# A hybrid attention and convolution layer on one core: the order of work at the end of each pair of column blocks, and one pattern of quads

## The chip, the cores and the metric

The kernel runs on one core of a Trainium2 chip. The metric is the device time of one execution in microseconds. A core has five engines that matter here: TensorE (PE) multiplies, VectorE (DVE) and ScalarE (ACT) work on elements, GpSimd (POOL) and SyncE (SP) issue transfers. Each engine takes its instructions from one queue, strictly in order: an instruction that waits holds up all that stand behind it.

## The reference

One layer on 256 tokens of width 4096, in float32, batch 1:

```python
u = rmsnorm(h, norm_gain)
proj = u @ w_in                                   # 4096 x 16384
q, k, v, z_a, hc, b_gate, c_gate, z_c = split(proj)   # each 2048 wide
attn  = moba_attention(q, k, v, rel_bias) * silu(z_a)          # 16 heads of 128
conv  = b_gate * short_conv(c_gate * hc, conv_w) * silu(z_c)   # causal, width 3, by channel
mixed = concatenate([attn, conv])
out   = rmsnorm(h + mixed @ w_out, final_gain)    # w_out 4096 x 4096
```

The attention's blocks are 256 long, and so is the sequence: each query sees the keys of its own block alone. What is left is causal attention over 256 tokens with a bias by distance.

## The kernel before

**Products.** 128 tokens are the rows of one matmul's output, so there are two token halves. The input projection has 32 column blocks of 512, taken two at a time: 16 pairs (numbers 0 to 15). Pairs 0 to 7 give q and k, then v and z_attn, in turn for four groups of heads; pairs 8 to 15 give h and C, then z_conv and B, for four groups of channels. The output projection adds 4 pairs (16 to 19). A pair goes through the 4096 contraction rows in 16 **quads** of 256 rows. The raw weights of a quad are 256 rows x two blocks of 512 columns: a tile `raw` of 128 x 2048, 1 MB.

A quad is one of two kinds. An **eight-quad** (`P` in a pattern) multiplies two token halves x two row halves x two column blocks: eight products. A **seven-quad** (`S`) uses Strassen's seven products instead: four of them take the raw blocks, three take sums of blocks, which L593 and L594 form on DVE in a tile `sum` of 128 x 1536. For the seven-quad, the sums of the activations stand ready in the tiles `k`. The first of the sums, block one plus block two, is formed in DRAM by a copy and an adding transfer that POOL issues (L528, L529), some quads ahead.

**Three passes.** Every operand is split into a high part, rounded to the format fp32r, and a low part, the rest. ACT casts the high part of the weights (`hi`, L611); DVE subtracts it for the low part (`lo`, L613). A product is three matmuls of 128 x 128 by 512 columns: high times high (L685), low activations times high weights (L686), high activations times low weights (L688). The low part is thus needed last, and within a unit all high products stand ahead of the low ones.

**Units.** A seven-quad is two units: the *raw unit* (12 matmuls) and the *sum unit* (9 matmuls). An eight-quad is one unit of 24 matmuls. `split(u + 2)` prepares the unit after next while unit u multiplies; three buffers each exist for `raw`, `hi` and `lo`. The program states what depends on what, and a scheduler sets the order in each engine's queue from it; it may move an instruction ahead of another of the same engine where nothing forbids it.

**The order of a pair.** `PATS` and `KIND` say which quads of a pair are seven-quads. Pairs 2 to 10, 12 and 14 have pattern `t`, which is `PSSPSSSPSSPSSSPP`: ten seven-quads in runs of two, three, two and three, the last at place 13, then two eight-quads.

**Accumulators.** PE writes into eight banks, 1 to 8 (odd pairs swap the names). The seven-quads' products go into all eight: banks 2, 3, 4 and 8 are the four results, and the banks 1, 5, 6 and 7 belong to shared products that have to be added to the results later. After the last seven-quad of a pair these four banks are done, and `early` evacuates them:

```python
es = cur["es"] = ep.tile([P, 4, B], F32, name="es")
nc.scalar.copy(es[:, 0], acc[1])                                                    # L395, ACT
nc.vector.tensor_tensor(es[:, 1], acc[6], es[:, 0], ALU.add)                        # L396, DVE
nc.vector.tensor_tensor(es[:, 2], acc[7], es[:, 1], ALU.add)                        # L397, DVE
nc.vector.tensor_tensor(es[:, 1::2], acc[5][:, None, :].to_broadcast([P, 2, B]), es[:, 1:3], ALU.subtract)  # L398, DVE
```

**What runs in the banks set free.** While the last two eight-quads fill banks 2, 3, 4 and 8, smaller work goes into banks 1, 5, 6 and 7, each piece counted in by products (`tasks_of`). In pairs 1, 3, 5 and 7 it is turning q and k (L300 on PE, L302 on ACT), the scores (L307 on PE, L313 the exponential on ACT) and turning the probabilities (L322, L324). In pairs 2, 4, 6 and 8 it is the values (L331 on PE, L336 on DVE) and turning what comes of them (L357 on PE, L358 on ACT). In pairs 10, 12 and 14 it is the convolution: PE turns the two inputs of a channel group (L377, L379), ACT takes the first tap, DVE the two others (L383) and the product (L385). In pair 17 it is one load of ACT's table for the square root (L655, L656). At the pair's end the results are taken out of banks 2, 3, 4 and 8 (L408 for the input pairs), with what `early` left in `es` added.

**The end of the program.** The last output pair finishes one token half after the other: `last_end` adds a quarter (L483) and squares it (L485), `summed` reduces the squares, and `finish` scales the half's 4096 columns and stores them (from L250 on).

Of the kernel before, what the change touches and what calls it, by code (L numbers as in the profile page):

```python
# [10 lines left out]
F32 = mybir.dt.float32  # L11
# [3 lines left out]
ALU = mybir.AluOpType  # L15
AX = mybir.AxisListType

P = 128
# [10 lines left out]
B = 512  # L29
# [8 lines left out]

PATS = {"7": "PSPSPSPSPSPSPSPP", "8": "PSPSSPSPSSPSPSPP", "n": "PSPSPSPSSPSPSPSP",
        "9": "PSPSSPSSPSSPSSPP", "m": "PSPSSPSPSSPSPSSP", "e": "PSPSPSPSPSPSSPPP", "f": "PSPSSPSPSSPSSPPP",  # L40
        "t": "PSSPSSSPSSPSSSPP"}
KIND = "01tttttt" "ttt9t9t9" "099e"
RING = 3
SLOT = 4
# [27 lines left out]
N_PAIRS = 16  # L72
# [11 lines left out]
def of(pattern):  # L84
    seven = SEVEN[:pattern.count("S")]
    eight = dict.fromkeys(EIGHT + SEVEN[len(seven):])
    return in_order(pattern, seven, [q for q in eight if q not in seven]), set(seven)
# [3 lines left out]
ORDERS, SEVENS = zip(*([(FIRST0, {8, 10, 12, 14}), (SECOND, {4, 6, 8, 10, 12, 14})]  # L91
                       + [of(PATS[k]) for k in KIND[2:N_PAIRS]]
                       + [(FIRST, {8, 6, 10, 12, 14})] + [of(PATS[k]) for k in KIND[N_PAIRS + 1:]]))
# [21 lines left out]
def hymba_layer(ctx: ExitStack, tc: tile.TileContext, xT, xres, gain, w, convw, wout,  # L115
                relb, onehot, fgain, out):
    nc = tc.nc
# [274 lines left out]
    def early(acc):  # L392

        es = cur["es"] = ep.tile([P, 4, B], F32, name="es")
        nc.scalar.copy(es[:, 0], acc[1])  # L395
        nc.vector.tensor_tensor(es[:, 1], acc[6], es[:, 0], ALU.add)  # L396
        nc.vector.tensor_tensor(es[:, 2], acc[7], es[:, 1], ALU.add)  # L397
        nc.vector.tensor_tensor(es[:, 1::2], acc[5][:, None, :].to_broadcast([P, 2, B]), es[:, 1:3], ALU.subtract)  # L398

    def part(t, n):  # L400
        return cur["es"][:, 2 * (1 - t) + n]
# [46 lines left out]
    def gain_load(p):  # L448
        gf = fin["gf"] = ep.tile([P, 8, P], F32, name="c", bufs=2).rearrange("p n c -> p (n c)")
        nc.sync.dma_start(gf, bass.AP(tensor=fgain.tensor, offset=fgain.offset + p * 2 * B,  # L450
                                      ap=[[0, P], [1, 2 * B]]))
# [4 lines left out]
    def pair_of(t):  # L456
        return cur["es"][:, 2 * (1 - t):2 * (2 - t)].rearrange("p n c -> p (n c)")

    def out_early(p, acc):
        early(acc)  # L460
        if p == NDP - 1:
            for t in (0, 1):
                added(p, t)
        gain_load(p)
# [6 lines left out]
    def added(p, t):  # L471
        nc.vector.tensor_tensor(row_of(p, t), row_of(p, t), pair_of(t), ALU.add)
# [34 lines left out]


    quads = QUADS
    raws, xrs, halves, sums, kept_at = {}, {}, {}, {}, []  # L510
    t1_d = [dram.tile([COPY, P * B // COPY], F32, name=f"t1_{j}") for j in range(T1S)]
    t1s, t1_next = {}, [0]

# [59 lines left out]
    def split(u):  # L573

        n, kind, at, products = units[u]
        first = u == 0 or units[u - 1][0] != n
        p, i, q = quads[n]
        if first:
            load(n + AHEAD)
            if p == 0:  # L580
                x_parts(q, xrs.pop(q))
            if q in SEVENS[p]:
                raw = raws[n].rearrange("p (b c) -> p b c", b=4)

                k = sum(x in SEVENS[p] for x in ORDERS[p][:i])
                if k % 2 and N_PAIRS <= p < N_PAIRS + NDP - 1:
                    t = fin["hg"][:, 0, D - 3 * B:].rearrange("p (b c) -> p b c", b=3)
                else:
                    t = (cur["pool"] if k % 2 and p < N_PAIRS else wp).tile([P, 3, B], F32, name="sum")
                sums[n] = t  # L590
                if n not in PRE:
                    nc.vector.tensor_tensor(raw[:, 0], raw[:, 0], raw[:, 1], ALU.add)
                nc.vector.tensor_tensor(t[:, 0], raw[:, 0], raw[:, 2], ALU.subtract)  # L593
                nc.vector.tensor_tensor(t[:, 1:], raw[:, 1::2], t[:, :1].to_broadcast([P, 2, B]), ALU.subtract)  # L594
        src = raws[n] if kind == "raw" else sums[n].rearrange("p b c -> p (b c)")
        m = len(products) * B
        src = src[:, at * B:at * B + m]
        if p == N_PAIRS + NDP - 1 and i >= KEPT:

            spot = ORDERS[p][2 * len(kept_at):]  # L600
            kept_at.append(u)
            hi, lo = (kt.tile([P, SIZES[k], 2, P], F32R, name=f"k{k}")
                      .rearrange("p n h c -> p (n h c)") for k in spot[:2])
        else:
            hi = wp.tile([P, SLOT * B], F32R, name="hi", bufs=RING)
            lo = wp.tile([P, SLOT * B], F32R, name="lo", bufs=RING)
        step = B if n < LEAD else m if m < 4 * B else LO * B
        for a in range(0, m, step):
            half = step if step < 2 * HI * B else HI * B
            for b in range(a, a + step, half):  # L610
                nc.scalar.copy(hi[:, b:b + half], src[:, b:b + half])  # L611
            c = slice(a, a + step)
            nc.vector.tensor_tensor(lo[:, c], src[:, c], hi[:, c].bitcast(F32), ALU.subtract)  # L613
        halves[u] = hi, lo


    def tasks_of(p):

        t = {}

        def put(at, f, *a):
            t.setdefault(at, []).append((f, a))
        if p < 8 and p % 2:
            for at, f, j, n in ((4, turn, 0, 1), (5, turn, 1, 6), (7, scores, 0, 7), (8, scores, 1, 5),
                                (9, turn, 2, 1), (11, probs, 0, 6), (12, turn, 3, 7), (13, scores, 2, 5),
                                (14, probs, 1, 1), (15, scores, 3, 6)):
                put(at, f, p // 2 * HG + j, n)
        elif 2 <= p <= 8:
            for j, (at, banks) in enumerate(zip(((4, 8), (6, 10), (8, 12), (11, 14)),
                                                ((1, 7), (6, 1), (5, 5), (7, 6)))):  # L630
                for f, a_, n in zip((values, mixed), at, banks):
                    put(a_, f, (p - 2) // 2 * HG + j, n)
        elif p == N_PAIRS + 1:

            put(8, root_table)
        elif p in (10, 12, 14):
            for j in range(4):
                put(4 + 3 * j, conv, (p - 10) // 2 * 4 + j, (7, 5, 1, 6)[j])
        return t
# [23 lines left out]
    acc = {}  # L663
# [27 lines left out]
    for u, (n, kind, at, products) in enumerate(units):  # L691
        p, i, q = quads[n]
# [10 lines left out]
        hi, lo = halves.pop(u)  # L703
# [28 lines left out]
        if i == last_seven[p]:  # L732
            assert not tasks
            behind, tasks = 0, tasks_of(p)
            if p < N_PAIRS:
                early(acc)
                rows = (rQ if p < 8 and p % 2 == 0 else rT, rT)
                for j, (_, t, c) in enumerate(ENDS):
                    tasks.setdefault(TS[j] if i < NQ - 2 else 4 + j, []).append((scaled, (part(t, c), rows[c][:, t:t + 1])))
            else:  # L740
                out_early(p - N_PAIRS, acc)

            split(u + 2)
        if (p, i) == (N_PAIRS + NDP - 2, NQ - 1):
# [9 lines left out]
        if (p, i + 1) in RAISE:  # L754
            q = RAISE[p, i + 1]
            raised[q] = x_again(q) if p < N_PAIRS else m_load(q)
        if (p, i) in RAISE:
            q = RAISE[p, i]
# [92 lines left out]
```

## Time and profile before

| | |
|---|---|
| time, median of 3 runs | 1708.32 us (1707.31 to 1709.75) |
| the profiled execution's own time | 1707.3 us |
| its span in the trace | 1705.5 us |
| PE busy | 1680.9 us, 7529 matmuls and transposes |
| DVE busy | 1562.0 us, 1348 instructions |
| ACT busy | 1064.8 us, 1182 instructions |
| POOL busy | 137.9 us, 173 instructions |
| moved by DMA | 458.91 MB, 269 GB/s on average |
| granted TensorE clock | 0.998 |

How to read the lines that follow. A row of the timeline gives the start in microseconds from the span's beginning, the length, the engine, the line of the kernel, the operation, what is written and read (a tile's name; `p` is a bank), the shape, the type, and how many alike follow one another; the length is from the first one's start to the last one's end. In square brackets stands the idle time of the engine just before, and what ended it. A matmul's recorded length overlaps the next one's: what a matmul takes of PE is read from one start to the next. Groups of instructions are rows of the page: the idle time before them, with the number of cases and the longest, stands behind what released them.

### The profile page before, as it was taken

What the parts mean: (1) busy time and instruction counts of PE and PEld (TensorE: products, weight loads), DVE (VectorE), ACT (ScalarE), POOL (GpSimd) and SP (SyncE); (2) the same over time, 40 slices, a digit from 0 to 9 for tenths busy, and PEclk for the clock granted to TensorE, in tenths of its full rate; (3) what the DMA queues carried; (4) which work ended last, traced back from release to release, by engine and by line L of the source; (5) the groups of instructions that cost most, each with busy time, mean ns of one, the idle gap of its engine ahead of it and who ended that gap; (6) DMA issues with size and microseconds to landing.
All of it is one profiled execution on the core that took longest, in us unless ns stands there. A gap on an engine that the chain in (4) does not pass through costs nothing.

```text
span 1705.5 us, 20704 instructions
## 1 busy us (share of the span) xinstructions
PE 1680.9 (99%) x7529; PEld 1382.5 (81%) x7529; DVE 1562.0 (92%) x1348; ACT 1064.8 (62%) x1182; POOL 137.9 (8%) x173
## 2 busy tenths in 40 slices
PE   9999999999999999999999999999999999999997
PEld 7888778888787878788888788888888888878886
DVE  7989988998899989899999999899989999989887
ACT  6856755675567556765665566656665656556563
POOL 0000000000000001010100001000100000001000
PEclk9999999999999999999999999999999999999999
DMA  9878788878797979797979798798888888889884
GB/s 335 296 249 290 228 263 261 270 249 287 242 288 231 282 244 282 230 283 245 292 257 291 239 281 271 250 292 268 272 261 274 283 308 294 275 276 277 284 292 171
DMA packets 119042, 458.91 MB, mean 269 GB/s; under 512 B 15499, under 2 KB 20396, under 8 KB 96940
## 3 DMA queue, kind: packets, MB, share of 16 engines
q1 hardware_dynamic: 94604, 413.66, 66.9%
q0 software_dynamic: 24048, 43.79, 15.9%
q8 instruction: 59, 0.97, 0.2%
q14 instruction: 43, 0.35, 0.1%
q10 hardware_dynamic: 288, 0.15, 0.0%
HBM read 448.36 MB, written 96.73 MB: 320 GB/s over the span
## 4 chain that ended last, share of the span: by engine, by line
PE 92%; DVE 4%; ACT 2%; issue 1%; DMA 1%; SPq 0%; DVEq 0%; ACTq 0%
PE p L685 30%; PE p L686 30%; PE p L688 30%; DVE lo L613 1%; DMA raw<-in_w_dram 1%; ACT hi L611 1%; DVE y L383 0%; ACT bt L313 0%; DVE es L397 0%; ACT L313 0%; DVE es L396 0%; DVE es L398 0%; PE p L307 0%; PE p L322 0%; PE p L331 0%
## 5 line engine op out<-in xcount | busy, mean ns | idle before, releaser
L685 PE MATMUL p<-hi,k 128*128 128x512 f32 x2359 | 918.5, 391 | 5.5 <-DVE mt L385 3.8
L686 PE MATMUL p<-hi,k 128*128 128x512 f32 x2359 | 915.9, 390 | 0.0
L613 DVE TENSOR_TENSOR lo<-raw,hi 128x2048 fp32r<-128x2048 f32 (+1 forms) x323 | 725.2, 2248 | 57.6 <-ACT hi L611 57.4
L611 ACT CAST hi<-raw 128x1024 fp32r<-128x1024 f32 (+1 forms) x638 | 635.3, 1042 | 209.9 <-PE p L686 139.9
L688 PE MATMUL p<-lo,k 128*128 128x512 f32 x2359 | 634.6, 392 | 0.0
L685 PEld LDWEIGHTS p<-hi,k 128*128 128x128 f32 x2359 | 442.8, 188 | 102.4 <-ACT hi L611 4.4
L686 PEld LDWEIGHTS p<-hi,k 128*128 128x128 f32 x2359 | 443.1, 188 | 91.9 <-issue 0.6
L688 PEld LDWEIGHTS p<-lo,k 128*128 128x128 f32 x2359 | 440.5, 188 | 88.8
L611 ACT CAST hi<-sum 128x1536 fp32r<-128x1536 f32 x167 | 247.5, 1482 | 279.6 <-DVE sum L594 211.6
L613 DVE TENSOR_TENSOR lo<-sum,hi 128x1536 fp32r<-128x1536 f32 x167 | 292.8, 1753 | 16.6 <-ACT hi L611 15.0
L529 POOL DMA_DIRECT2D t<-in_w_dram x137 | 112.6, 822 | 1208.3 <-DMA t<-in_w_dram 880.3
L594 DVE TENSOR_TENSOR sum<-raw,sum 128x1024 f32<-128x1024 f32 x167 | 204.2, 1223 | 3.4
L593 DVE TENSOR_TENSOR sum<-raw 128x512 f32<-128x512 f32 x167 | 114.5, 686 | 0.6 <-DMA raw<-in_wout_dram 0.4
L396 DVE TENSOR_TENSOR es<-p,es 128x512 f32<-128x512 f32 x20 | 13.8, 691 | 41.6 <-PE p L688 31.9
L404 ACT ACTIVATE es<-es,rT 128x512 f32<-128x512 f32 x56 | 39.5, 721 | 14.4 <-DVE es L398 12.1
L529 POOL DMA_DIRECT2D t<-in_wout_dram x30 | 24.6, 821 | 293.9 <-DMA t<-in_wout_dram 227.7
L395 ACT COPY es<-p 128x512 f32<-128x512 f32 x20 | 11.7, 587 | 48.7 <-PE p L688 48.6
L611 ACT CAST hi<-hg 128x1536 fp32r<-128x1536 f32 x10 | 14.8, 1481 | 25.7 <-DVE hg L594 20.9
L175 DVE TENSOR_TENSOR k<-c,k 128x128 fp32r<-128x128 f32 (+3 forms) x42 | 25.5, 627 | 3.4 <-ACT k L174 3.4
L174 ACT CAST k<-c 128x128 fp32r<-128x128 f32 (+3 forms) x42 | 22.9, 567 | 3.5 <-DVE c L171 3.5
L398 DVE TENSOR_TENSOR es<-p,es 128x1024 f32<-128x1024 f32 x20 | 24.4, 1220 | 0.2
L171 DVE TENSOR_TENSOR c<-c 128x128 f32<-128x128 f32 x76 | 18.8, 287 | 0.1
(112 smaller groups left out, 525.3 us busy)
## 6 DMA issues: line engine op xcount, KB each, us to landing
raw<-in_w_dram SPq DMA_DIRECT2D x117, 1024.0 KB, 6.9
raw<-in_w_dram SPq DMA_DIRECT2D x137, 768.0 KB, 5.9
raw<-t SPq DMA_DIRECT2D x167, 256.0 KB, 3.6
t<-in_w_dram SPq DMA_DIRECT2D x137, 256.0 KB, 6.0
t<-in_w_dram POOLq DMA_DIRECT2D x137, 256.0 KB, 6.1
raw<-in_wout_dram SPq DMA_DIRECT2D x34, 1024.0 KB, 6.1
raw<-in_wout_dram SPq DMA_DIRECT2D x30, 768.0 KB, 6.4
t<-in_wout_dram SPq DMA_DIRECT2D x30, 256.0 KB, 7.0
```

The lines of the kernel that those rows point to most:

```text
L174: nc.scalar.copy(dst[:, :, 0], c)
L175: nc.vector.tensor_tensor(dst[:, :, 1], c, dst[:, :, 0].bitcast(F32), ALU.subtract)
L398: nc.vector.tensor_tensor(es[:, 1::2], acc[5][:, None, :].to_broadcast([P, 2, B]), es[:, 1:3], ALU.subtract)
L404: nc.scalar.activation(e, e, AF.Copy, scale=r)
L529: nc.gpsimd.dma_start(by_rows(t1), rest[:, :B], accum_op=ALU.add)
L593: nc.vector.tensor_tensor(t[:, 0], raw[:, 0], raw[:, 2], ALU.subtract)
L594: nc.vector.tensor_tensor(t[:, 1:], raw[:, 1::2], t[:, :1].to_broadcast([P, 2, B]), ALU.subtract)
L611: nc.scalar.copy(hi[:, b:b + half], src[:, b:b + half])
L613: nc.vector.tensor_tensor(lo[:, c], src[:, c], hi[:, c].bitcast(F32), ALU.subtract)
L685: nc.tensor.matmul(acc[b_], a, h_, start=s0, stop=False)
L686: nc.tensor.matmul(acc[b_], b, h_, start=False, stop=False)
L688: nc.tensor.matmul(acc[b_], a, l_, start=False, stop=s1)
```

## The change

Three things are altered; no instruction is added or removed on any engine.

1. In every seven-quad both sums (L593, L594) are put ahead of the raw unit's low part, by keeping the second sum and the low part in the order in which the program states them. (Lines of the changed kernel from here on: 592, 593, 612 for the cast, 614 for the low part.)
2. `split` remembers the last cast and the last low part of each unit. `early` is issued behind those of the unit that follows the last seven-quad (the first of the two eight-quads): on ACT L395 stands behind that unit's cast, on DVE L396 to L398 behind its low part.
3. Pattern `t` has its run of two and its second run of three exchanged: `PSSPSSSPSSSPSSPP`. The ten seven-quads and the six eight-quads are the same in number; the last seven-quad is still at place 13, with one seven-quad ahead of it instead of two.

```diff
-        "t": "PSSPSSSPSSPSSSPP"}
+        "t": "PSSPSSSPSSSPSSPP"}
...
-    def out_early(p, acc):
-        early(acc)
+    def out_early(p):
...
-                nc.vector.tensor_tensor(t[:, 1:], raw[:, 1::2], t[:, :1].to_broadcast([P, 2, B]), ALU.subtract)
+                made = nc.vector.tensor_tensor(t[:, 1:], raw[:, 1::2], t[:, :1].to_broadcast([P, 2, B]),
+                                               ALU.subtract)
+                tc.keep_in_program_order(made)
...
-                nc.scalar.copy(hi[:, b:b + half], src[:, b:b + half])
+                cast = nc.scalar.copy(hi[:, b:b + half], src[:, b:b + half])
             c = slice(a, a + step)
-            nc.vector.tensor_tensor(lo[:, c], src[:, c], hi[:, c].bitcast(F32), ALU.subtract)
+            low = nc.vector.tensor_tensor(lo[:, c], src[:, c], hi[:, c].bitcast(F32), ALU.subtract)
+            if kind == "raw" and q in SEVENS[p]:
+                tc.keep_in_program_order(low)
         halves[u] = hi, lo
+        ends[u] = cast.ins, low.ins
...
         if i == last_seven[p]:
             assert not tasks
             behind, tasks = 0, tasks_of(p)
+            with tc.issue_after(ends[u + 1][0]), tc.issue_after(ends[u + 1][1]):
+                early(acc)
             if p < N_PAIRS:
-                early(acc)
...
             else:
-                out_early(p - N_PAIRS, acc)
+                out_early(p - N_PAIRS)
```

**DVE at the end of pair 2.** `lo_2055` is the low part of the last seven-quad's sum unit, `lo_2070` and `lo_2106` are those of the two eight-quads behind it, `es` is the evacuation, and the rows of L336 are the heads' values. Before:

```order
L613 TENSOR_TENSOR lo_2055<-sum_2034,hi_2054 128x1536
L396 TENSOR_TENSOR es_2095<-p6_1653,es_2095 128x512
L336 SCALAR_TENSOR_TENSOR am_2144<-p1_2140,st_1471,z_1570 128x128
L397 TENSOR_TENSOR es_2095<-p7_1656,es_2095 128x512
L336 SCALAR_TENSOR_TENSOR am_2144<-p1_2140,st_1471,z_1570 128x128
L398 TENSOR_TENSOR es_2095<-p5_1635,es_2095 128x2x512
L336 SCALAR_TENSOR_TENSOR am_2154<-p6_2150,st_1482,z_1570 128x128 x2
L613 TENSOR_TENSOR lo_2070<-raw_1996,hi_2069 128x2048
```

In the changed kernel:

```order
L614 TENSOR_TENSOR lo_2055<-sum_2034,hi_2054 128x1536
L614 TENSOR_TENSOR lo_2070<-raw_1983,hi_2069 128x2048
L396 TENSOR_TENSOR es_2095<-p6_1653,es_2095 128x512
L397 TENSOR_TENSOR es_2095<-p7_1656,es_2095 128x512
L398 TENSOR_TENSOR es_2095<-p5_1635,es_2095 128x2x512
L336 SCALAR_TENSOR_TENSOR am_2144<-p1_2140,st_1471,z_1570 128x128 x2
L336 SCALAR_TENSOR_TENSOR am_2154<-p6_2150,st_1482,z_1570 128x128
L614 TENSOR_TENSOR lo_2106<-raw_2032,hi_2105 128x2048
```

The low part of the first eight-quad has gone from behind the evacuation to ahead of it, and the three instructions of the evacuation stand together, without the first head's values between them.

**DVE at the end of pair 12**, from the first two channel groups' products (L385 of `mt_8573`) to those of the other two (`mt_8633`). `sum_8597`, `lo_8601` belong to the first seven-quad of the next pair. Before:

```order
L385 TENSOR_TENSOR mt_8573<-p5_8579,y_8584 128x256
L593 TENSOR_TENSOR sum_8597<-raw_8527 128x512
L613 TENSOR_TENSOR lo_8601<-raw_8527,hi_8600 128x2048
L594 TENSOR_TENSOR sum_8597<-raw_8527,sum_8597 128x1024
L383 SCALAR_TENSOR_TENSOR y_8629<-p1_8624,cw_71,y_8629 128x255
L383 SCALAR_TENSOR_TENSOR y_8644<-p6_8639,cw_71,y_8644 128x255
L383 SCALAR_TENSOR_TENSOR y_8629<-p1_8624,cw_71,y_8629 128x254
L383 SCALAR_TENSOR_TENSOR y_8644<-p6_8639,cw_71,y_8644 128x254
L385 TENSOR_TENSOR mt_8633<-p1_8624,y_8629 128x256
L385 TENSOR_TENSOR mt_8633<-p6_8639,y_8644 128x256
```

In the changed kernel:

```order
L385 TENSOR_TENSOR mt_8573<-p5_8579,y_8584 128x256
L592 TENSOR_TENSOR sum_8597<-raw_8527 128x512
L383 SCALAR_TENSOR_TENSOR y_8629<-p1_8624,cw_71,y_8629 128x255
L593 TENSOR_TENSOR sum_8597<-raw_8527,sum_8597 128x1024
L614 TENSOR_TENSOR lo_8601<-raw_8527,hi_8600 128x2048
L383 SCALAR_TENSOR_TENSOR y_8629<-p1_8624,cw_71,y_8629 128x254
L383 SCALAR_TENSOR_TENSOR y_8644<-p6_8639,cw_71,y_8644 128x255
L385 TENSOR_TENSOR mt_8633<-p1_8624,y_8629 128x256
L383 SCALAR_TENSOR_TENSOR y_8644<-p6_8639,cw_71,y_8644 128x254
L408 SCALAR_TENSOR_TENSOR s_8654<-p3_8030,rT_69,es_8522 128x512
L385 TENSOR_TENSOR mt_8633<-p6_8639,y_8644 128x256
```

The second sum now stands ahead of the raw low part, both lie between the third group's taps, and one of the pair's results (L408) has come ahead of the last product.

**ACT at the end of pair 17**, where a table load follows the evacuation. `hi_11651` is the cast of the last seven-quad's sum unit, `hi_11666` that of the first eight-quad. Before:

```order
L611 CAST hi_11651<-sum_11631 128x1536
L395 COPY es_11692<-p2_11246 128x512
L655 ACTIVATE spare_102<-es_11692 128x1
L656 ACT_TABLE_LOAD
L656 ACTIVATE spare_102<-spare_102 128x1
L611 CAST hi_11666<-raw_11583 128x1024 x2
```

In the changed kernel:

```order
L612 CAST hi_11651<-sum_11631 128x1536
L612 CAST hi_11666<-raw_11583 128x1024 x2
L395 COPY es_11692<-p2_11246 128x512
L659 ACTIVATE spare_102<-es_11692 128x1
L660 ACT_TABLE_LOAD
L660 ACTIVATE spare_102<-spare_102 128x1
```

The cast has gone from behind the copy and the table load to ahead of both.

More of the change, by code (lines that the diff above doesn't have):

```diff
@@ L509, in hymba_layer @@
     quads = QUADS
-    raws, xrs, halves, sums, kept_at = {}, {}, {}, {}, []
+    raws, xrs, halves, sums, kept_at, ends = {}, {}, {}, {}, [], {}
     t1_d = [dram.tile([COPY, P * B // COPY], F32, name=f"t1_{j}") for j in range(T1S)]
```

## The prediction

> **What bounds the kernel now.** I read the page's busy times, then the waits, then the order of time around each end of a pair.
>
> ```profile
> PE 1680.9 (99%) x7529; PEld 1382.5 (81%) x7529; DVE 1562.0 (92%) x1348; ACT 1064.8 (62%) x1182; POOL 137.9 (8%) x173
> ```
> ```profile
> 774.02 0.39 PE L685 MATMUL p<-hi,k 128*128 128x512 f32 x1
> ...
> 777.65 1.07 PE L688 MATMUL p<-lo,k 128*128 128x512 f32 x4
> ...
> 779.00 0.39 PE L333 MATMUL p<-v,pt 128*128 128x128 f32 x2
> 779.14 0.71 PE L688 MATMUL p<-lo,k 128*128 128x512 f32 x2
> ```
> PE sets the time. Sixteen 512-column matmuls start between 774.02 and 777.65, so one takes 0.227 us of PE; a 128-column pair takes 0.14 (779.00 to 779.14). The change removes no matmul, so it can only win PE's waits. Those sit at ends of pairs, where the accumulators that the seven-products filled are evacuated:
>
> ```profile
> DVE es L396 <- PE p L688: 31.9, 13, 4.0
> ```
> Here DVE stands with the evacuation at the head of its queue and waits for PE, 13 times and up to 4.0 us. Call the last seven-quad's sum unit u, the two eight-quads after it u+1 and u+2, and T0 the time at which PE could start u+1. The end of pair 2, PE first, then ACT, then DVE:
>
> ```profile
> 252.85 0.38 PE L333 MATMUL p<-v,pt 128*128 128x128 f32 x2
> 253.40 0.49 PE L331 MATMUL p<-v,pt 128*128 128x128 f32 x2 [0.17 <-DVE es L396]
> ...
> 254.28 0.59 PE L357 MATMUL p<-ident,am 128*128 128x128 f32 x2
> 255.76 0.46 PE L331 MATMUL p<-v,pt 128*128 128x128 f32 x2 [0.89 <-DVE es L398]
> ```
> ```profile
> 250.97 0.59 ACT L395 COPY es<-p 128x512 f32<-128x512 f32 x1 [3.82 <-PE p L688]
> ...
> 254.01 1.98 ACT L611 CAST hi<-raw 128x1024 fp32r<-128x1024 f32 x2
> ```
> ```profile
> 252.66 0.69 DVE L396 TENSOR_TENSOR es<-p,es 128x512 f32<-128x512 f32 x1 [3.52 <-PE p L688]
> ...
> 256.04 2.28 DVE L613 TENSOR_TENSOR lo<-raw,hi 128x2048 fp32r<-128x2048 f32 x1
> ```
> ACT idles 3.82 us and DVE 3.52, while u+1's high part (254.01) and low part (256.04) are queued behind. PE fills in with attention products, which need the banks that L396 to L398 free, and waits twice: 0.55 instead of 0.14 after 252.85, and 1.48 instead of 0.28 (two passes at 0.14) after 254.28. That is 0.4 + 1.2 = **1.6 us** per such place.
>
> **The change part by part.** *Evacuation behind u+1's parts, even pairs 2, 4, 6.* Pair 8 of the kernel before already stands in the order that the change gives these pairs (low part of u+1 ahead of L396):
>
> ```profile
> 770.87 2.29 DVE L613 TENSOR_TENSOR lo<-raw,hi 128x2048 fp32r<-128x2048 f32 x1
> 773.84 0.69 DVE L396 TENSOR_TENSOR es<-p,es 128x512 f32<-128x512 f32 x1 [0.68 <-PE p L688]
> ```
> ```profile
> 768.83 2.01 ACT L611 CAST hi<-raw 128x1024 fp32r<-128x1024 f32 x2 [0.30 <-PE p L686]
> ```
> The cast and the 2.29 us low part fill the wait, L396 still waits 0.68 us for PE, so it isn't late, and PE passes without a stall: after its attention products (779.00) the next low product starts 0.14 later. I take 1.6 us for pairs 2, 4 and 6 (4 and 6 issue the same tasks): 3 x 1.6 = **-4.8**. Bounds: 0 where the wait only moves on to the bank's next user, -4.8 where it goes.
>
> *Pair 17.* ACT holds u+1's cast behind L395 and a table load; PE waits for the cast:
>
> ```profile
> 1518.18 0.84 PE L688 MATMUL p<-lo,k 128*128 128x512 f32 x3
> 1520.35 0.50 PE L685 MATMUL p<-hi,k 128*128 128x512 f32 x1 [1.32 <-ACT hi L611]
> ```
> T0 is 1518.18 + 3 x 0.227 = 1518.86, so 1.49 is lost. In the new order the cast stands ahead of L395: **-1.5**, or 0 if the raw data come late.
>
> *Convolution pairs 12 and 14.* PE's new pair waits for the banks that the convolution heads read last (L385):
>
> ```profile
> 1103.58 0.84 PE L688 MATMUL p<-lo,k 128*128 128x512 f32 x3
> ...
> 1121.31 0.47 PE L685 MATMUL p<-hi,k 128*128 128x512 f32 x1 [0.70 <-DVE mt L385]
> ```
> ```profile
> 1104.08 0.69 DVE L396 TENSOR_TENSOR es<-p,es 128x512 f32<-128x512 f32 x1 [3.03 <-PE p L688]
> ...
> 1113.02 1.65 DVE L383 SCALAR_TENSOR_TENSOR y<-p,cw,y 128x255 f32<-128x255 f32 x4
> 1114.59 0.75 DVE L385 TENSOR_TENSOR mt<-p,y 128x256 f32<-128x256 f32 x2
> 1115.25 0.68 DVE L593 TENSOR_TENSOR sum<-raw 128x512 f32<-128x512 f32 x1
> 1115.85 2.29 DVE L613 TENSOR_TENSOR lo<-raw,hi 128x2048 fp32r<-128x2048 f32 x1
> 1118.05 1.22 DVE L594 TENSOR_TENSOR sum<-raw,sum 128x1024 f32<-128x1024 f32 x1
> ```
> T0 is 1104.26 and the wait ends 17.05 us later. The low part moved into the 3.03 us hole frees 2.2 us of DVE, but the gain doesn't pass on whole: PE now transposes the second head only after 8 low and 10 high products of u+1 and u+2 and the first head (0.5): T0 + 3.63 + 18 x 0.227 + 0.5 = 1112.5. Its transposes (0.5) and ACT's part (0.5) bring DVE to 1113.5. From there in the new order: three L383 (1.2), two L385 (0.7), L593 (0.6), one L383 (0.4), L594 (1.1), the low part (2.2), two L383 (0.8), one L385 (0.4): 1120.9. The wait ended at 1121.31, so it is 0.3 shorter; pair 14 is alike: **-0.6** together. Bounds: +1 (a slower second head), and -1.6 if the waits go.
>
> *Convolution pair 10.* In the queue before, its two last heads' transposes are hoisted into u:
>
> ```profile
> 937.59 0.38 PE L377 MATMUL p<-ident,s 128*128 128x128 f32 x2
> ...
> 957.26 0.50 PE L685 MATMUL p<-hi,k 128*128 128x512 f32 x1 [2.27 <-DVE mt L385]
> ```
> Without the hoist T0 is 937.59 + 0.68 = 938.27, and PE gets to the same block 18.99 us after it. The new order there is pair 12's, for which I have 1121.0 - 1104.26 = 16.7. **-2.3**; bounds 0 and -2.9.
>
> *Score pairs 3, 5, 7.* Their new order is the one that pair 1 already has (turns behind u+1's high products):
>
> ```profile
> 163.37 0.84 PE L688 MATMUL p<-lo,k 128*128 128x512 f32 x3
> ...
> 180.24 0.70 PE L307 MATMUL p<-qk 128*128 128x256 f32 x2 [1.02 <-ACT qk L302]
> ```
> ```profile
> 337.60 0.38 PE L300 MATMUL p<-ident,q 128*128 128x128 f32 x2
> ...
> 353.91 0.70 PE L307 MATMUL p<-qk 128*128 128x256 f32 x2 [0.52 <-ACT qk L302]
> ```
> ```profile
> 170.66 0.71 ACT L174 CAST k<-c 128x128 fp32r<-128x128 f32 x2
> ```
> Pair 1 needs 180.24 - 164.05 = 16.19 from T0 to the third head's scores, with 0.6 us of ACT casts (170.66) that pair 3 lacks: 15.6. Pair 3 needs 353.91 - 338.28 = 15.63 now. So 0.0: both wait for ACT's softmax and copies. Bounds +0.6 each if pair 1's time holds whole, -1 each if PE's waits go.
>
> *Sums ahead of the raw low part, and the moved run.* The same instructions, each queue's total unchanged. An S quad costs DVE about 0.6 + 1.1 + 2.2 + 1.7 = 5.6 us against 21 x 0.227 = 4.8 on PE, an eight-quad 2.2 against 5.4: a run of three loses 2.5 and one eight-quad wins it back. The sum's cast comes up to 2.2 us earlier, the raw low part up to 1.1 later. PE shows no wait inside runs: I take 0. POOL's queue stays in order; SP's loads move with the quads, and a raw buffer comes free earlier at u+1.
>
> *The end.* The third output quarter's sum (L483) now goes behind the first token half's scaling:
>
> ```profile
> 1690.68 0.69 DVE L483 TENSOR_TENSOR hg<-p,hg 128x512 f32<-128x512 f32 x1 [0.95 <-PE p L688]
> 1691.29 0.15 DVE L250 RECIPROCAL rf<-rs_s 128x1 f32<-128x1 f32 x1
> ```
> ```profile
> 1691.41 0.63 ACT L485 ACTIVATE es<-hg 128x512 f32<-128x512 f32 x1 [1.44 <-DVE hg L483]
> ```
> Now the scaling (from L250) starts after that L483 and its 0.95 us of wait; in the new order L483 and its square on ACT (0.63) come after the scaling, and the reduction for the second token half, which needs the square, ahead of the last L483. The scaling starts between 0.6 us (L483 alone, 1690.68 to 1691.29) and 1.6 us (with the wait) earlier, and 0.6 + 0.6 + 0.1 come between it and the last L483: the end moves by -0.3 to +0.7, and I take **+0.3**.
>
> Sum: -4.8 - 1.5 - 0.6 - 2.3 + 0 + 0.3 = **-8.9**. The profiled execution's span 1705.5 becomes 1696.6, its 1707.3 becomes 1698.4; the median 1708.32 becomes **1699.4**.
>
> [...]
>
> **The rivals.** (a) *The banks are what is scarce*: the next user of a bank meets the wait again, whatever the queue's order. Then only pairs 10 and 17 gain: 1708.3 - 3.8 = 1704.5. For it: eight accumulators and four evacuated banks that every task reuses; against it: pair 8. [...] Chance 0.17, half of it with no gain beyond 0.2%.
>
> (b) *The raw low part becomes late*, the case on the other side. In pair 3's run of three:
>
> ```profile
> 298.49 2.28 DVE L613 TENSOR_TENSOR lo<-raw,hi 128x2048 fp32r<-128x2048 f32 x1
> ```
> ```profile
> 301.33 1.07 PE L688 MATMUL p<-lo,k 128*128 128x512 f32 x4
> ```
> it ends 0.56 us ahead of its product. A second run of three now follows after one eight-quad; if that doesn't refill the lead, the second run lacks 2.5 - 0.5 = 2 us in each of nine such pairs: 1699.4 + 18 = 1717. It decides from the point where the lead after the eight-quad is below 2.5 us. Against it: 3.2 us are won there. Chance 0.07.
>
> (c) *More goes than I count*: the score pairs' waits too, and pairs 12 and 14 whole: another 4 us, 1695.4. Chance 0.14.
>
> **How the numbers follow.** Forecast 0.62, (a) 0.17, (b) 0.07, (c) 0.14. A measurement of this kernel can tell 0.2%, or 3.4 us: faster is below 1704.9. Faster 0.62 + 0.14 + half of (a) 0.08 = 0.84; same 0.10 with a little from (b); slower 0.06. The range 1694.5 to 1705.5 holds the forecast, (c) and the better part of (a).
>
> **What would show it.** Right: at the ends of pairs 2, 4, 6 L331 without a wait for L396 or L398, DVE's hole ahead of L396 filled by a low part; the waits for L385 at 0.3; no wait for a cast in pair 17; PE's busy time shorter. Wrong: new waits of PE's low products for the raw low part inside runs of seven-quads, or the even pairs' waits back at another bank; a wait in the score pairs over 2 us.

## The result, and the profile after

The changed kernel takes **1696.62 us** (median; 1696.22 to 1697.53), the kernel before 1708.14 on the same chip. The ratio is 0.9932, with a 95% interval of 0.9915 to 0.9949: 0.7% faster, where 0.2% can be told. The forecast was 1699.4 us (1694.5 to 1705.5). The profiled executions moved less than the medians, 1707.3 to 1697.5, since that of before is the fastest of its runs and that of the changed kernel the slowest; further down too, what is said of single pairs is of one execution, up to 2.2 us from its kernel's median. By their spans, 1705.5 and 1695.7, the change is worth 9.8 us, where 8.9 was forecast.

The page of the changed kernel, busy times and three groups of instructions:

```profile
PE 1678.0 (99%) x7529; PEld 1382.5 (82%) x7529; DVE 1566.4 (92%) x1348; ACT 1070.7 (63%) x1182; POOL 137.9 (8%) x173
...
L689 PE MATMUL p<-hi,k 128*128 128x512 f32 x2359 | 917.2, 390 | 1.6 <-DVE mt L385 1.3
...
L692 PE MATMUL p<-lo,k 128*128 128x512 f32 x2359 | 636.8, 392 | 0.5 <-DVE lo L614 0.5
...
L396 DVE TENSOR_TENSOR es<-p,es 128x512 f32<-128x512 f32 x20 | 13.8, 690 | 11.4 <-PE p L692 10.5
```

The first and the last of these groups in the kernel before:

```profile
L685 PE MATMUL p<-hi,k 128*128 128x512 f32 x2359 | 918.5, 391 | 5.5 <-DVE mt L385 3.8
...
L396 DVE TENSOR_TENSOR es<-p,es 128x512 f32<-128x512 f32 x20 | 13.8, 691 | 41.6 <-PE p L688 31.9
```

DVE now idles 11.4 us ahead of L396, where it idled 41.6. PE's first high products (L689) wait 1.6 us in all, where they waited 5.5. Something new is there: low products (L692) wait 0.5 us for their low part.

The end of pair 2 in the changed kernel's timeline, PE, then DVE, then ACT:

```profile
252.00 0.84 PE L692 MATMUL p<-lo,k 128*128 128x512 f32 x3
252.68 0.39 PE L689 MATMUL p<-hi,k 128*128 128x512 f32 x1
...
257.21 0.38 PE L331 MATMUL p<-v,pt 128*128 128x128 f32 x2
...
258.34 0.38 PE L331 MATMUL p<-v,pt 128*128 128x128 f32 x2
```
```profile
249.51 2.29 DVE L614 TENSOR_TENSOR lo<-raw,hi 128x2048 fp32r<-128x2048 f32 x1 [0.75 <-ACT hi L612]
252.49 0.69 DVE L396 TENSOR_TENSOR es<-p,es 128x512 f32<-128x512 f32 x1 [0.69 <-PE p L692]
```
```profile
247.48 2.00 ACT L612 CAST hi<-raw 128x1024 fp32r<-128x1024 f32 x2 [0.51 <-PE p L690]
251.29 0.59 ACT L395 COPY es<-p 128x512 f32<-128x512 f32 x1 [1.81 <-PE p L692]
```

The cast and the low part of the next unit lie in the holes ahead of L395 and L396. PE goes from the last low product of the sum unit (three from 252.00) straight to the next unit's high products (252.68), and takes the values 4.5 us later (257.21), when L398, the last of the evacuation, has been over for 2.0 us. L396 still waits for PE, so it isn't late.

To add up the parts, I cut both traces at the same matmuls: from the one at 40% of a pair's 512-column matmuls to the one at 40% of the next pair's. Each stretch then holds one pair's end. What the changed kernel differs by, in us:

| end of pair | forecast | measured |
|---|---|---|
| 2, 4, 6 | -4.8 | -1.94, -2.01, -1.99 = -5.9 |
| 17 | -1.5 | -1.6 |
| 12, 14 | -0.6 | -0.22, -0.47 = -0.7 |
| 10 | -2.3 | -1.1 |
| 3, 5, 7 | 0 | -0.06, -0.40, -0.11 = -0.6 |
| after PE's last matmul | +0.3 | -0.1 |
| the start, to the middle of pair 2 | 0 | +0.3 |
| all others | 0 | -0.1 |
| sum | -8.9 | -9.8 |

### The profile page after: what moved, and what is told of

Its sections match the earlier page's. It is cut to its first block, busy times and chain, and to the rows that moved or that the text cites. A ratio compares the mean times of both kernels' runs of the same rounds, so it can differ in the third digit from the quotient of the medians.

```text
span 1695.7 us, 20681 instructions
## 1 busy us (share of the span) xinstructions
PE 1678.0 (99%) x7529; PEld 1382.5 (82%) x7529; DVE 1566.4 (92%) x1348; ACT 1070.7 (63%) x1182; POOL 137.9 (8%) x173
## 4 chain that ended last, share of the span: by engine, by line
PE 94%; ACT 2%; DVE 2%; DMA 1%; issue 0%; SPq 0%; DVEq 0%; ACTq 0%
PE p L689 31%; PE p L690 31%; PE p L692 31%; ACT hi L612 1%; DMA raw<-in_w_dram 1%; DVE lo L614 1%; DVE y L383 0%; ACT es L404 0%; ACT qk L302 0%; ACT bt L313 0%; ACT L313 0%; DVE sum L593 0%; PE p L307 0%; PE p L322 0%; PE p L333 0%
## 5 line engine op out<-in xcount | busy, mean ns | idle before, releaser
L689 PE MATMUL p<-hi,k 128*128 128x512 f32 x2359 | 917.2, 390 | 1.6 <-DVE mt L385 1.3
L692 PE MATMUL p<-lo,k 128*128 128x512 f32 x2359 | 636.8, 392 | 0.5 <-DVE lo L614 0.5
L689 PEld LDWEIGHTS p<-hi,k 128*128 128x128 f32 x2359 | 443.0, 188 | 97.8 <-issue 2.5
L692 PEld LDWEIGHTS p<-lo,k 128*128 128x128 f32 x2359 | 440.2, 188 | 89.8 <-DVE lo L614 1.3
L593 DVE TENSOR_TENSOR sum<-raw,sum 128x1024 f32<-128x1024 f32 x167 | 204.2, 1223 | 4.9
L395 ACT COPY es<-p 128x512 f32<-128x512 f32 x20 | 11.7, 587 | 23.9 <-PE p L692 23.8
L398 DVE TENSOR_TENSOR es<-p,es 128x1024 f32<-128x1024 f32 x20 | 24.4, 1218 | 0.2
L396 DVE TENSOR_TENSOR es<-p,es 128x512 f32<-128x512 f32 x20 | 13.8, 690 | 11.4 <-PE p L692 10.5
L336 DVE SCALAR_TENSOR_TENSOR am<-p,st,z 128x128 f32<-128x128 f32 x32 | 9.6, 343 | 12.4 <-PE p L333 10.1
```

Source lines behind the costliest of these rows:

```text
L593: made = nc.vector.tensor_tensor(t[:, 1:], raw[:, 1::2], t[:, :1].to_broadcast([P, 2, B]), ALU.subtract)
L689: nc.tensor.matmul(acc[b_], a, h_, start=s0, stop=False)
L692: nc.tensor.matmul(acc[b_], a, l_, start=False, stop=s1)
```

## The experiments

The theory: PE loses time at the ends of pairs because the evacuation stands at the heads of ACT's and DVE's queues, ahead of work that could be done already. First each part was tried alone. The three labels with `only` are the kernel before plus one part, `no_sums`, `no_pat` and `no_evac` the changed kernel less one part. All ratios are against runs of the kernel before on the same chip.

**The pattern alone.**

```diff
-        "t": "PSSPSSSPSSPSSSPP"}
+        "t": "PSSPSSSPSSSPSSPP"}
```

> The kernel before with the third part alone: pattern t has its second run of three ahead of its run of two; the evacuation and the sums stand as before. Theory (the time goes at the evacuation's place in the queues of ACT and DVE): the waits of the even pairs' values (0.3 and 1.1 us each), of pair 17 (1.5 us) and of pair 10 stay, so the time stays at 1706 to 1710 us. Rival (the run of two ahead of the pair's end lets DVE arrive there earlier, and this carries the gain): half of it or more, below 1703 us. Second rival (the second run of three after one eight-quad lacks DVE time): PE's low products wait for the raw low part inside it, 2 us in each of nine pairs, 1715 us or more.

Measured: 1702.09 us against 1708.9, ratio 0.9960 (0.9948 to 0.9973). The theory missed: the pattern alone brings 6.8 us. Its timeline at the end of pair 2:

```profile
253.66 0.49 PE L331 MATMUL p<-v,pt 128*128 128x128 f32 x2 [0.17 <-DVE es L396]
253.91 0.48 PE L685 MATMUL p<-hi,k 128*128 128x512 f32 x1
...
259.00 0.38 PE L332 MATMUL p<-v,pt 128*128 128x128 f32 x2
```
```profile
252.92 0.69 DVE L396 TENSOR_TENSOR es<-p,es 128x512 f32<-128x512 f32 x1 [4.18 <-PE p L688]
...
254.65 2.28 DVE L613 TENSOR_TENSOR lo<-raw,hi 128x2048 fp32r<-128x2048 f32 x1
256.85 1.22 DVE L398 TENSOR_TENSOR es<-p,es 128x1024 f32<-128x1024 f32 x1
```

The wait for L396 is still there, the 1.1 us for L398 are gone, though L398 now ends at 258.07, later than before (255.8 at the most, when the value waiting for it began). DVE still waits 4.18 us at L396. Two queues have moved: with the other pattern the scheduler puts the next unit's sixteen high products ahead of the third value on PE, and the next unit's low part (254.65) ahead of L398 on DVE. The second rival's lack of DVE time in the second run of three isn't there. The first rival is right in size, but not in its reason: DVE does come to L396 earlier, and only waits the longer for PE, 4.18 us instead of 3.52. Pairs 2, 4 and 6 gain 1.4 us each, 3, 5 and 7 1.1 together, pair 10 0.8, and pair 12 loses 0.8.

**The evacuation alone**, the same edit as in the change (`issue_after` around `early`).

> The kernel before with the second part alone: the evacuation stands behind the next unit's cast and low part; the sums and pattern t as before. Theory: nearly the whole gain. The waits of the values in pairs 2, 4 and 6 go (6 us with the small ones around them), pair 17's goes (1.6), the waits for L385 in pairs 10, 12 and 14 fall to about 0.6, and the wait of 0.69 us for a raw low part in pair 11, which the changed kernel shows, is not there, since this low part doesn't stand behind two sums: 1696 to 1697.5 us. Rival (the parts need one another, since the low part is ready in time only with the other pattern or the earlier sums): 1701 us or more, with new waits for the low part.

Measured: 1697.02 us, ratio 0.9930 (0.9917 to 0.9942). As the theory had it: the second part is worth the whole gain by itself, and what the pattern brings is some of the same waits taken away in another way. The parts don't add. The new place has a price that the theory left out, in pair 16, where PE waits for the last of the evacuation and 1.1 us are lost (nothing in the changed kernel):

```profile
1440.64 0.47 PE L686 MATMUL p<-hi,k 128*128 128x512 f32 x1 [0.90 <-DVE es L398]
```

**Sums first alone.**

```diff
+                tc.keep_in_program_order(made)
...
+            if kind == "raw" and q in SEVENS[p]:
+                tc.keep_in_program_order(low)
```

> The kernel before with the first part alone: both sums ahead of the raw low part. Theory: nothing at the ends of the pairs, apart from the order of the third token quarter's end, 1707 to 1710 us. Rival (the sum's cast comes earlier, so the sum unit's parts are never late, and that is where time went): 1704 us or less. Second rival (the raw low part now stands behind two sums of 1.8 us together and is late): 1711 us or more, with waits of low products for it.

Measured: 1711.2 us, ratio 1.0015 (1.0006 to 1.0024): slower, by little. In its trace pairs 10 and 12 lose 1.4 and 1.0 us, pair 17 2.1. In pair 10 a low product waits for the raw low part as the second rival says, but the wait for L385 right behind it falls from 2.27 us to 0.62:

```profile
956.56 0.49 PE L692 MATMUL p<-lo,k 128*128 128x512 f32 x1 [1.01 <-DVE lo L614]
957.67 0.50 PE L689 MATMUL p<-hi,k 128*128 128x512 f32 x1 [0.62 <-DVE mt L385]
```

Up to there nothing is lost against the kernel before. The pair's loss comes after it, and like 1.4 of pair 17's it is a thing of its own, which the last section takes up. Pair 17:

```profile
1524.63 0.50 PE L689 MATMUL p<-hi,k 128*128 128x512 f32 x1 [1.78 <-ACT hi L612]
...
1526.41 0.63 PE L690 MATMUL p<-hi,k 128*128 128x512 f32 x1
1526.83 0.63 PE L689 MATMUL p<-hi,k 128*128 128x512 f32 x1
```

**The change without sums first.**

> The changed kernel without its first part: the evacuation's new place and the other pattern, the sums free to stand where the scheduler puts them. Theory: the same as the changed kernel within 1.5 us, 1695 to 1697; the wait of 0.69 us in pair 11 goes. Rival (the sums' place is what keeps the sum unit's parts in time in the second run of three): 1700 us or more.

Measured: 1695.53 us, ratio 0.9922 (0.9909 to 0.9936). Its runs (1695.33 to 1696.21) lie below all of the changed kernel's, though they come from another series. The gain is in the convolution pairs: pair 10 moves by -1.8 us against before (-1.1 in the changed kernel), pairs 12 and 14 by -1.0 and -1.1 (-0.2 and -0.5). The changed kernel, behind pair 10 on PE and DVE:

```profile
963.86 0.50 PE L692 MATMUL p<-lo,k 128*128 128x512 f32 x1 [0.53 <-DVE lo L614]
```
```profile
957.14 0.68 DVE L592 TENSOR_TENSOR sum<-raw 128x512 f32<-128x512 f32 x1
959.77 0.69 DVE L592 TENSOR_TENSOR sum<-raw 128x512 f32<-128x512 f32 x1 [1.95 <-DMA raw<-in_w_dram]
960.38 1.22 DVE L593 TENSOR_TENSOR sum<-raw,sum 128x1024 f32<-128x1024 f32 x1
961.51 2.29 DVE L614 TENSOR_TENSOR lo<-raw,hi 128x2048 fp32r<-128x2048 f32 x1
```

The raw low part stands behind two first sums, the second of which waits 1.95 us for a load. Without sums first, the low part stands directly behind the first one:

```profile
957.09 0.68 DVE L592 TENSOR_TENSOR sum<-raw 128x512 f32<-128x512 f32 x1
957.69 2.28 DVE L613 TENSOR_TENSOR lo<-raw,hi 128x2048 fp32r<-128x2048 f32 x1
```

In pair 12 it is PE's queue again. The changed kernel turns the second channel group at 1105.27 and waits for L385 in the end. Without sums first it does so at 1103.16, of which 0.7 us were won before this pair and 1.4 here, and there is no wait:

```profile
1105.27 0.38 PE L377 MATMUL p<-ident,s 128*128 128x128 f32 x2
...
1113.92 0.47 PE L689 MATMUL p<-hi,k 128*128 128x512 f32 x1 [0.49 <-DVE mt L385]
```
```profile
1103.16 0.38 PE L377 MATMUL p<-ident,s 128*128 128x128 f32 x2
```

**The change without the other pattern.**

> The changed kernel with the old pattern t: sums first, evacuation at its new place. Evacuation alone gave 1697.0 us, the changed kernel 1696.6, the changed kernel without sums first 1695.5. Theory (with the evacuation at its new place the pattern adds nothing; sums first costs DVE's order in the convolution pairs 2 us): 1696 to 1699 us, with the waits for L385 as in the changed kernel. Rival (the pattern keeps a share of its own 6.8 us beside the evacuation): 1700 us or more.

Measured: 1697.48 us, ratio 0.9938 (0.9926 to 0.9951), as the theory expected. Beside the evacuation's new place the pattern is worth nothing that can be told.

**The change without the evacuation's place.**

> The changed kernel without its second part: sums first and the other pattern, the evacuation where the scheduler puts it. The pattern alone gave 1702.1 us (1.4 us in each of pairs 2, 4 and 6), sums first alone 1711.2, against 1708.9. Theory (the pattern works through the order that the scheduler then gives PE and ACT at the end of an even pair, and sums first costs what it costs alone): 1702 to 1706 us, with a wait of 0.3 us for L396 in the even pairs, and none for L398. Rival (the evacuation's place alone decides, and the pattern's gain was an accident of that run's order): 1708 us or more.

Measured: 1704.29 us, ratio 0.9981 (0.9972 to 0.9989), in the theory's range: the pattern's gain in the even pairs stays (1.4 us each, and the wait of 0.17 us for L396 as in `pat_only`), and sums first costs some 2 us, as it does alone, with the wait of 1.78 us in pair 17 again; pair 10 loses nothing by it here.

**The evacuation one unit further back.**

```diff
-            with tc.issue_after(ends[u + 1][0]), tc.issue_after(ends[u + 1][1]):
+            split(u + 2)
+            with tc.issue_after(ends[u + 2][0]), tc.issue_after(ends[u + 2][1]):
                 early(acc)
...
-            split(u + 2)
```

> The changed kernel with the evacuation one unit further back: behind the cast and the low part of the second eight-quad too. Worked out from the changed kernel's trace, L396 then starts about 1.6 us later in pair 2 and L398 ends some 0.4 us ahead of the first value that needs a bank. Theory (the banks have slack, the queue's head was the trouble): 1695 to 1699 us. Rival (banks are scarce, the new place is just early enough): each of 13 pairs waits for the evacuation again, about 1 us each, 1706 us or more.

Measured: 1709.45 us, ratio 1.0009 (1.0000 to 1.0018): the whole gain is lost, 12.8 us against the changed kernel's median (9.3 between the two traces). The theory's figure was far off and the rival's size is right, though not its place. Against the changed kernel, the even pairs lose only 0.6 or 0.7 us each; their banks do have slack. The score pairs lose 0.9, 0.9 and 2.5, some 1.6 of the last by what the last section tells, and the convolution pairs 0.6, 1.5 and 1.1. Pair 10 shows how, on PE and DVE:

```profile
937.53 0.84 PE L692 MATMUL p<-lo,k 128*128 128x512 f32 x3
...
946.15 0.38 PE L377 MATMUL p<-ident,s 128*128 128x128 f32 x2
...
954.65 0.47 PE L689 MATMUL p<-hi,k 128*128 128x512 f32 x1 [2.21 <-DVE mt L385]
```
```profile
939.71 0.68 DVE L396 TENSOR_TENSOR es<-p,es 128x512 f32<-128x512 f32 x1
```

L396 starts 1.5 us after the sum unit's last product (938.21), and the first channel group is turned only 7.9 us after it, where the changed kernel turns it 4.8 us after (936.92, the last product over at 932.15). What follows a turn is a chain through ACT and DVE (L381, L383, L385), four times over; begun that late, it doesn't end before the next pair. So of the three places tried, ahead of the next units' parts, behind one unit's and behind two, the change has the best.

**Only ACT's scaling behind the cast**, in the kernel before. Is it the late cast that PE lacks in the even pairs, or PE's own order?

```diff
-        nc.scalar.activation(e, e, AF.Copy, scale=r)
+        with tc.issue_after(behind_):
+            nc.scalar.activation(e, e, AF.Copy, scale=r)
```

> The kernel before with one thing altered: on ACT the scaling of the evacuated quarters (L404) stands behind the next unit's cast, so that in pairs 2, 4 and 6 the cast (254.01 in the trace of before) starts right after L395, 2 us earlier. PE's and DVE's orders stay as they are. Theory (PE's own queue decides: the heads' values that need L396 and L398 stand ahead of the next unit's high products): no gain, 1707 to 1710 us, the waits of 0.3 and 1.1 us as before. Rival (the late cast is what PE lacks): 1.4 us less in each of three pairs, about 1704.5 us.

Measured: 1709.89 us, ratio 1.0009 (1.0000 to 1.0018): no gain. The cast comes 2.3 us earlier, and PE's values wait as before:

```profile
251.73 2.00 ACT L612 CAST hi<-raw 128x1024 fp32r<-128x1024 f32 x2
```
```profile
253.69 0.49 PE L331 MATMUL p<-v,pt 128*128 128x128 f32 x2 [0.17 <-DVE es L396]
...
256.04 0.35 PE L331 MATMUL p<-v,pt 128*128 128x128 f32 x1 [0.89 <-DVE es L398]
```

**PE's order as well**, the evacuation still ahead of the low part on DVE.

```diff
+            cur["high"] = nc.tensor.matmul(acc[b_], b, h_, start=False, stop=False)
...
-                        f(*args)
+                        with tc.issue_after(cur["high"].ins) if f in (values, mixed) else nullcontext():
+                            f(*args)
```

> The kernel before with the scaling behind the cast (as in the run before, which gained nothing) and, besides, PE's products of the heads' values in pairs 2, 4, 6 and 8 behind the high products of the unit in hand. PE's order there becomes that of the changed kernel; the evacuation is not moved, so on DVE L396 to L398 still stand ahead of the next unit's low part. Theory (PE's queue is what cost 2.0 us in each even pair, but the low part must come ahead of the evacuation too): the waits for L396 and L398 go, and a new wait of about 1 us for the low part comes, since it ends at 257.5 and is wanted 3.6 us after PE starts the unit, at 256.5: 1 us less in each of three pairs, 1704 to 1707 us. Rival (PE's order alone is enough): 2 us less in each, 1702 to 1703 us, and no wait for the low part. Second rival (nothing gained): 1708 us.

Measured: 1708.16 us, ratio 0.9997 (0.9988 to 1.0006): nothing gained, as the second rival had it, though by the theory's mechanism. The waits for L396 and L398 are gone, and one for the low part has come:

```profile
256.41 0.39 PE L688 MATMUL p<-hi,k 128*128 128x512 f32 x1
257.45 1.20 PE L690 MATMUL p<-lo,k 128*128 128x512 f32 x4 [0.65 <-DVE lo L614]
```
```profile
253.98 1.22 DVE L398 TENSOR_TENSOR es<-p,es 128x1024 f32<-128x1024 f32 x1
255.12 2.28 DVE L614 TENSOR_TENSOR lo<-raw,hi 128x2048 fp32r<-128x2048 f32 x1
```

An even pair gains 0.5 us of the 2.0, where I had said 1; the score pairs lose 0.8 in all and the end 0.6. Pair 10 is 1.6 longer in this trace by the slow matmuls of the last section (granted clock 0.54 over 3.5 us). Together with `pat_only`, where the low part came ahead of L398 as well and an even pair gained 1.4, this run tells what the place of the evacuation does in the even pairs. It has to change two queues at once: PE's, so that high products stand ahead of the values, and DVE's, so that the low part is ready when the high products end.

**The evacuation behind the low part on DVE only.**

```diff
-            with tc.issue_after(ends[u + 1][0]), tc.issue_after(ends[u + 1][1]):
+            with tc.issue_after(ends[u + 1][1]):
```

> The changed kernel with the evacuation behind the next unit's low part on DVE only; on ACT L395 is free to stand ahead of the cast. Theory (ACT's queue counts where something slow follows L395, or where DVE's low part then comes late): pair 17 waits 1.5 us for its cast again, the low part comes 2.7 us later at the pairs' ends, 1698 to 1703 us. Rival (DVE's order carries all): 1696 to 1697 us, as the changed kernel.

Measured: 1702.83 us, ratio 0.9966 (0.9954 to 0.9978), in the theory's range, 6 us behind the changed kernel. Pairs 2, 4 and 6 keep nearly all of their gain (1.8 or 1.9 us each). Pair 17 is 3.7 us longer than in the changed kernel, 1.6 of it by the slow matmuls of the last section (two of them start at 1516.76 and 1517.19, 0.43 us apart), and the convolution pairs 1.5 together:

```profile
1515.46 0.50 PE L689 MATMUL p<-hi,k 128*128 128x512 f32 x1 [1.78 <-ACT hi L612]
```

So ACT's half of the edit is worth its share where something slow follows L395 (the table load of 1.28 us in pair 17), DVE's half in the even pairs. Why the convolution pairs lose without ACT's half is not shown.

**A version that goes on.** Sums first left out; and in pairs 1, 3, 5 and 7 the scalings ahead of the first head's copy, L398 ahead of the second eight-quad's low part, and the turned heads' copies behind the last exponential issued.

```diff
-        nc.scalar.copy(QK[h], ps)
+        with tc.issue_after(cur["scaled"].ins), tc.issue_after(cur.get("exp", cur["scaled"]).ins):
+            nc.scalar.copy(QK[h], ps)
...
+                    if odd:
+                        scaled(part(t, c), rows[c][:, t:t + 1])
+                        continue
...
-            split(u + 2)
+            with tc.issue_after(last_early.ins) if odd else nullcontext():
+                split(u + 2)
```

> A version that goes on from the changed kernel without sums first (1695.5 us). What is left at the ends of pairs 1, 3, 5 and 7 is PE's wait of 1.0 to 1.2 us for the third head's copy (L302), which stands on ACT behind the scaling of the evacuated quarters, a table load and two heads' exponentials, while ACT idles 3.5 us earlier, ahead of the first head's copy. The edit, in these four pairs alone: L398 ahead of the second eight-quad's low part on DVE, the four scalings ahead of the first head's copy on ACT, and the third head's copy behind the second head's exponential. Theory (ACT's queue decides, and 1.3 us of scaling taken out of it ends the wait): 1691 to 1693.5 us. Rival (the wait passes on to the exponentials, or to the first head's copy, which now stands behind the scaling): 1694.5 us or more.

Measured: 1694.2 us (1694.16 to 1694.81), ratio 0.9916 (0.9902 to 0.9930). It is the fastest kernel here, 2.4 us below the changed one's median and 1.3 below `no_sums`, on which it builds, but it lies between the theory's range and the rival's. The 1 us of waiting for the third head's copy is down to 0.2. In pairs 5 and 7 a wait of about the same size stands behind it, for a bank that a head's scores still hold, and in pair 1 a longer one, for a bank out of which a result (L410 here) is taken later:

```profile
180.13 0.51 PE L688 MATMUL p<-hi,k 128*128 128x512 f32 x1 [1.77 <-DVE z L410]
...
523.94 0.50 PE L688 MATMUL p<-hi,k 128*128 128x512 f32 x1 [0.77 <-DVE bt L310]
```

Only pair 3 keeps its gain (1.2 us). In the other three the wait did pass on to the next user of a bank.

## Why the prediction was right, and where not

The direction, the mechanism and the range were right, and the sum of the terms missed the profiled span's change by 0.9 us, the median by 2.8. That the sum came so close is in part luck: the even pairs' term was too small by 1.1 and pair 10's too large by 1.2, and they cancel. Point by point:

- **Pairs 2, 4, 6** (forecast 3 x 1.6). The mechanism is shown by both sides: the waits go with the new order; ACT's part alone doesn't bring it (`scale_behind`), ACT's and PE's together bring 0.5 us of it (`pe_order`), and DVE's, which PE's order follows, 1.8 or 1.9 (`dve_half`). The size was too low, 2.0 each. I had summed the two rows with a wait; the rest is a tenth of a microsecond here and there around the broken-up attention products. Pair 8, my price for these places, would have told: cut at the same matmuls, the end of pair 8 took 83.97 us before, that of pair 2 85.93. That is 1.96.
- **Pair 17**: 1.6 for 1.5, and the wait comes back with ACT's half undone.
- **Pairs 12, 14**: 0.7 for 0.6, but the small figure hid two larger ones. The evacuation's place is worth 2.1 there (`evac_only`), and sums first costs 1.4 of it (`no_pat` gains 0.6).
- **Pair 10** is the place that failed: 1.1 for 2.3. Its own term held: the wait for L385 fell from 2.27 to 0.49 us, and at that product 2.1 us had been gained. Of these 1.0 was lost behind it, 0.7 at one low product of pair 11. So it is the step "Sums ahead of the raw low part, and the moved run ... I take 0" that was wrong behind a pair's end, where DVE has a backlog: the raw low part is late there, by 0.53 us. Without sums first nothing is lost behind the wait for L385 (`no_sums`). In `no_pat`, which has sums first, PE comes to that low product 0.5 us later and hardly waits, but passes it at the same moment, 963.80 against 963.86: the first sum ahead of the low part waits for its load there too, and starts at 959.71 against 959.77. So the load sets the time.
- **Pairs 3, 5, 7**: forecast 0, measured -0.6. The third head's wait ends 352.25 - 336.66 = 15.6 us after T0, just as I had worked out, and the wait of 0.28 us for L396 at the first heads' turns is gone. What I compared, the moment at which a wait ends, leaves out what PE has done by then.
- **The end**: +0.3 forecast, -0.1 measured. I had moved the scaling as if DVE set the time there. The last sum waits for PE anyway, so the order of what lies before it costs nothing:

```profile
1685.07 0.69 DVE L482 TENSOR_TENSOR hg<-p,hg 128x512 f32<-128x512 f32 x1 [0.46 <-PE p L692]
```

- **Rival (a)**, scarce banks, isn't what happened, but it isn't far off. One unit further back (`too_far`), with the wait for a copy gone (`hole_filled`), or in pair 16 with the evacuation alone (`evac_only`), the next user of a bank does decide.
- **Rival (b)**, the second run of three short of DVE time, never shows: `pat_only` and `no_sums` have no wait inside the runs. Its price was worked out wrongly too: pattern `t` stands in eleven pairs, not nine, so 2 us in each would have made 22 us, not 18.
- **Rival (c)**, more goes than I count: its half on pairs 12 and 14 is true as soon as the sums are left free, which gives 1695.5 us; its half on the score pairs isn't, their waits for L302 stay in every kernel but `hole_filled`.

What I had not considered is how much a moved run changes what the scheduler writes into PE's queue. I judged the pattern by DVE's balance and gave it 0; alone it is worth 6.8 us, though beside the evacuation's place nothing. For the sum it made no difference, since I had priced the whole new order at each place, not its parts.

## What to carry to other kernels

Where an engine stands at the head of its queue with work that can't start yet, look for work behind it that could, and put it ahead, but only as much as fits the hole: here one unit's parts gained 12 us (`evac_only`), and two units' parts lost it all again. A place where the program already stands in the new order is the best price list; take the whole stretch between two equal matmuls from it, not only the rows with a wait. And when several edits go together, each should be tried alone: the evacuation's place was the whole gain, the pattern repeated part of it, and sums first took a microsecond back.

## What the runs showed of the hardware

ACT took its instructions in the order of its queue: in pair 17 of the kernel before it idled 4.14 us ahead of L395 (1517.02), and the cast that stands behind it began at 1519.27; in the changed kernel, where this cast stands ahead, it began at 1505.59 and L395 at 1509.40. DVE's rows at the ends of pairs 2 and 12 too start in the order printed for its queue, in both kernels.

After some waits PE's matmuls started 0.43 us apart for a while, instead of 0.227, and the granted clock was 0.54 to 0.57 in windows over three such stretches. Windows of `sums_only` at pair 17 (columns: length, busy time and count of each engine, then the granted clock):

```profile
1526.00:1529.00 3.00, 3.00 (x9) 2.37 (x8) 3.00 (x2) 3.00 (x4) 0.00 (x0) 0.55 0.03 11
1529.00:1540.00 11.00, 11.00 (x51) 9.08 (x50) 8.41 (x7) 3.80 (x4) 0.84 (x1) 1.00 0.99 351
```

Seven matmuls there take 0.2 us extra each (two of the starts are 1526.41 and 1526.83, above): 1.4 us on top of a wait of 1.78. A slow stretch came behind the wait of 1.78 us in pair 17 in all three traces that have it (`sums_only`, `no_evac`, `dve_half`), behind two waits of 1.01 and 0.62 close together in pair 10 of `sums_only` (eight slow matmuls from 958.73, 0.2 us extra each), and behind one of 1.13 in pair 7 of `too_far` (five). But length doesn't decide: the wait of 2.27 us at the end of pair 10 in the kernel before has no slow matmuls behind it (granted clock 1.00 from 957.5 to 961), nor has one of 2.21 in `too_far`, and in `pe_order` one of 2.29 at the same place has eight:

```profile
957.50:961.00 3.50, 3.50 (x11) 2.67 (x10) 3.50 (x5) 0.85 (x1) 0.83 (x1) 0.54 0.74 260
```

Eleven matmuls are in this window, where the kernel before has 16 in the same one. Eight matmuls at 0.43 are 3.4 us. What decides whether a slow stretch follows a wait is not shown. In `sums_only` it cost 1.4 us in pair 17 and 1.6 in pair 10, on top of the waits. For the granted clock of a whole execution I estimate from the first window of `sums_only` that 3.4 us at 0.55, in some 1700 us, take off 3.4 x 0.45 / 1700, about 0.001. The spans of `no_evac` fit that: 1701.6 to 1703.2 us where it was 0.998 (seven executions), 1703.8 to 1704.3 at 0.997 (three), 1705.6 at 0.996 (one). How many stretches an execution without a trace had is not on record.
